# RWKV scan on one core: VectorE copies and scales for both heads, and the first two MLA weights get a pool of their own

## The chip, the core and the metric

The kernel runs on one core of a Trainium2 chip. A core has a matmul engine (TensorE, PE in the profile; PEld is its weight load), a vector engine (VectorE, DVE), a scalar engine (ScalarE, ACT), a general engine (GpSimd, POOL) and a sync engine (SyncE, SP) that here only issues DMAs. Each engine runs its own queue in order; engines wait for each other by semaphores. The metric is the device time of one execution in microseconds. Three executions of the kernel before gave a median of 4153.34 us (4151.22 to 4157.22).

## The reference, cut to what matters

Two networks run one after the other. The first has two hybrid layers; the second has four layers: an SGU mixer, an RWKV-7 mixer, an MLA attention mixer and another SGU mixer, over 512 tokens and 256 context tokens, width 1024. The change lies in the RWKV mixer's scan and at the start of the MLA mixer.

The reference's scan goes token by token in two directions (forward and flipped), 16 heads of 64 x 64 state:

```
def step(S, inp):
    w_t, k_t, v_t, kk_t, a_t = inp[:5]
    s_kk = einsum('nbhvk,nbhk->nbhv', S, kk_t)
    S = S * w_t[..., None, :] - s_kk[..., :, None] * (kk_t * a_t)[..., None, :] \
        + v_t[..., :, None] * k_t[..., None, :]
    y_t = einsum('nbhvk,nbhk->nbhv', S, inp[5])
```

MLA projects the normed hidden state `h` by columns of one matrix: `c_q, c_kv, k_rope, z = split(h @ w_in, ...)`, with 768 columns for `c_q` and then 256 for `c_kv`.

## The kernel before, in words

Everything is float32. Each weight is split into a high and a low part (`wtile`, L129): ScalarE casts (`whi`, L138), VectorE or every third time GpSimd subtracts (`wlo`, L141), and a product is three matmuls (L160).

**The scan** (`scan`, L1689). The tokens go in chunks of 64, twelve chunks (`NS`) for each of eight blocks of 128 channels (`KD`). One block holds two heads: head 0 on partitions 0 to 63, head 1 on 64 to 127, in both the VectorE inputs and the outputs. Two blocks are in flight, half a block apart: each iteration `p` of the outer loop (L1697) runs six steps of block `p` and the last six of block `p-1` side by side, two "lanes". Beside the lanes an iteration weaves in the products of the groups to come (`products`, L1774 to 1787: G, GR, TK), the triangular inverse of a later block (`inverse`, on GpSimd, L1810 to 1825, during the first iterations) with its `merge`, and the `output` of the block that was finished (L1946 to 1965, and then L160 and L999 for the output projection). PE's order there is fixed by the way the generators are woven; the other engines' orders are set by the framework's scheduler.

A lane's step (`step`, L1878): four 64-wide matmuls of G and SV (L1889); VectorE copies the result out of PSUM (`rh`, L1896); four matmuls with the inverse; their result, the chunk's update, is copied out of PSUM into `VU` (L1901 for head 0 on ScalarE, L1902 for head 1 on VectorE); four matmuls of TK and VU give the state's increment; VectorE forms the new state `st` (L1912, two instructions); the state times the next chunk's decay goes into `SV` (L1918 for head 0, two instructions on ScalarE; L1919 for head 1, one on VectorE); eight matmuls give `y`, which is copied or added into `yacc`. Both copies of a `VU` read one PSUM bank, and the framework makes L1902 wait for L1901.

The output chain: `yacc` is centred (L1949), squared on ScalarE (`ysq`, L1952), scaled (L1959), given gain and bias on ScalarE (L1961), then VectorE adds the bonus (L1963), multiplies by the gate (L1965), and after a cast on ScalarE (L177) forms the low part (L178).

**The MLA start** (`Mla.run`, L2007). Two weights of 1024 x 128 (`wkv`, L2041) come from the weight pool of the stage (two raw tiles, three high, two low). That pool is opened when the scan's pools are closed. Then `hidden` forms the normed hidden state (`hid`, `hh`, `hl`, L973 to 979, L177, L178), and the two weights multiply it.

Of the kernel before, what the change touches and what calls it, by code (L numbers as in the profile page):

```python
# [15 lines left out]
AF = mybir.ActivationFunctionType  # L16
ALU = mybir.AluOpType
# [1105 lines left out]
def flip(ap, dim):  # L1123

    a = [list(p) for p in ap.ap]
    st, n = a[dim]
    a[dim] = [-st, n]
    return bass.AP(tensor=ap.tensor, offset=ap.offset + st * (n - 1), ap=a)
# [60 lines left out]
class Rwkv:  # L1189
# [688 lines left out]
    def step(self, k, cur, s):  # L1878


        net, nc, ap = self.net, self.net.nc, self.ap
        g, q = s // 4, s % 4
        G, GR, TK, VU, SV = cur[g]
        h = [slice(0, 64), slice(64, 128)]
        de = [(d, e) for d in range(2) for e in range(2)]
        if s == 0:
            cur["y"] = ap.tile([128, S + C], F32, tag="yacc", name="yacc", bufs=3)
        TT, ps, py = cur["TT"], net.aux(), None
        mm = lambda o, d, e, a, b, first=False, last=True: nc.tensor.matmul(  # L1889
            (ps if o else py)[h[e], o * 128 + d * 64:o * 128 + d * 64 + 64], lhsT=a, rhs=b, start=first, stop=last, skip_group_check=True)  # L1890
        part = lambda o: (ps if o else py)[:, o * 128:o * 128 + 128].rearrange("p (d v) -> p d v", v=64)
        for d, e in de:
            mm(1, d, e, G[:, e, d, q, 0, :], SV[:, e, d, q, :], d == 0)
        yield
        rh = ap.tile([128, 2, 64], F32, tag="rh", name="rh", bufs=3)
        nc.vector.tensor_copy(rh, part(1))  # L1896
        yield
        for d, e in de:
            mm(2, d, e, TT[h[e], d, s, :], rh[h[e], d, :])
        yield  # L1900
        nc.scalar.copy(VU[h[0], 0, :, q, :], part(2)[h[0]])  # L1901
        nc.vector.tensor_copy(VU[h[1], 1, :, q, :], part(2)[h[1]])  # L1902
        yield
        if s < NS - 1:
            for d, e in de:
                mm(3, d, e, TK[:, e, d, q, :], VU[:, e, d, q, :])

            t = ap.tile([128, 2, 64], F32, tag="st", name="st", bufs=6)
            ec = self.ec[:, k, s]
            if s:  # L1910
                for d in range(2):
                    nc.vector.scalar_tensor_tensor(t[:, d], cur["st"][:, d], self.ec[:, k, s - 1, d:d + 1], part(3)[:, d], ALU.mult, ALU.add)  # L1912
            else:
                nc.vector.tensor_copy(t, part(3))
            cur["st"] = t
            to = cur[(s + 1) // 4][4]
            for d in range(2):
                nc.scalar.activation(to[h[0], 0, d, (s + 1) % 4, :], t[h[0], d], AF.Copy, scale=ec[h[0], d:d + 1])  # L1918
            nc.vector.tensor_tensor(to[h[1], 1, :, (s + 1) % 4, :], t[h[1]], ec[h[1], :, None].to_broadcast([64, 2, 64]), ALU.mult)  # L1919
        yield  # L1920
        py = net.aux()
        for d, e in de:
            mm(0, d, e, SV[:, e, d, q, :], G[:, e, d, q, 1, :], d == 0, False)
        for d, e in de:
            mm(0, d, e, VU[:, e, d, q, :], GR[:, d, q, e, :])
        for d in range(2):
            c = (8 + (s if d == 0 else 3 - s)) if s < 4 else (s - 4 if d == 0 else 11 - s)
            dst = cur["y"][:, c * 64:c * 64 + 64]
            if d:
                dst = flip(dst, 1)  # L1930
            if s in (2, 3) or s >= 8:
                nc.vector.tensor_tensor(dst, dst, part(0)[:, d], ALU.add)
            else:
                nc.scalar.copy(dst, part(0)[:, d])
        yield
# [65 lines left out]
class Mla:  # L2001
# [5 lines left out]
    def run(self):  # L2007
        net, nc, I, tc = self.net, self.net.nc, self.net.I, self.net.tc
# [4 lines left out]
        with ExitStack() as es:  # L2013
# [24 lines left out]
            krt = mp.tile([128, NT2, 64], F32, name="krt")  # L2038
            kr2 = mp.tile([128, NT2], F32, name="kr2")
            with net.weight_pool(2, 3, 2), net.psum(6, 2), tc.tile_pool(name="mla1", reuse_waits="tile", bufs=3) as ap:  # L2040
                wkv = [net.wcols(w_in[:, 768 + k * 128:896 + k * 128], 128) for k in range(2)]  # L2041
                hT = self.b2.hidden(i, ap, ap, True)

                raw = [ap.tile([128, T], F32, name=f"ckr{k}", bufs=1) for k in range(2)]
                for k in range(2):
                    outs = self.b2.both(True)
                    net.strip(outs, wkv[k], hT)
                    for ps, t0, t1 in outs:
                        nc.scalar.copy(raw[k][:, t0:t1], ps[:, :t1 - t0])

                outs = self.b2.both(True)
                net.strip(outs, net.wcols(w_in[:, 1024:1088], 64), hT, m=64)
                kr = ap.tile([64, T], F32, name="kr", bufs=1)
                krsq = ap.tile([64, T], F32, name="krsq", bufs=1)
                for ps, t0, t1 in outs:
                    nc.scalar.activation(kr[:, t0:t1], ps[:64, :t1 - t0], AF.Copy, scale=gr[0:64, 1:2])
                    nc.scalar.activation(krsq[:, t0:t1], ps[:64, :t1 - t0], AF.Square)
                ps = net.aux()
                for c in range(NT2):
                    nc.tensor.matmul(ps[:, c:c + 1], lhsT=krsq[:, c * 128:c * 128 + 128], rhs=net.ones[0:64, 0:1], start=True, stop=True)  # L2060
                nc.vector.tensor_copy(kr2, ps[:, :NT2])
                self.rotate(perm[0:64, 0:64], kr[:, 0:S], kr[:, 0:S], ap, 64, net.aux)
                ps = net.aux()
                for c in range(NT2):
                    nc.tensor.transpose(ps[:, c * 64:c * 64 + 64], kr[:, c * 128:c * 128 + 128], net.ident[0:64, 0:64])
                nc.scalar.copy(krt.rearrange("p c d -> p (c d)"), ps[:, :NT2 * 64])
                self.normed(raw, ckv, cols["kvn"], 256, ((0, NCH), (NCH, 2)), ap)
                rawq = [ap.tile([128, S], F32, name=f"cqr{k}", bufs=1) for k in range(6)]
                for k in range(6):
                    ps = net.acc()  # L2070
                    net.strip([(ps, 0, S)], net.wcols(w_in[:, k * 128:k * 128 + 128], 128), hT)
                    nc.scalar.copy(rawq[k], ps)
                for h in range(MH):
                    ps = net.acc()
                    net.strip([(ps, 0, S)], net.wcols(w_in[:, 1088 + h * 128:1216 + h * 128], 128), hT)
                    z = ap.tile([128, S], F32, tag="zs", name="zs", bufs=2)
                    nc.scalar.activation(z, ps, AF.Tanh, scale=0.5)
                    nc.vector.scalar_tensor_tensor(z, z, 1.0, ps, ALU.add, ALU.mult)
                    nc.sync.dma_start(zd[h * 128:h * 128 + 128, :], z)
                    if h == 0:  # L2080
                        self.normed(rawq, cq, cols["qn"], 768, ((0, NCH),), ap)
            net.drop_context()
            na, nb, nw, no = HEAD_BANKS
            with net.weight_pool(1, 3, 3), net.psum(na, nb, nw), tc.tile_pool(name="po", reuse_waits="tile", bufs=no, space=PSUM) as self.pv, \
# [382 lines left out]
```

## Time and profile before

| | |
|---|---|
| median of three executions | 4153.34 us |
| the profiled execution | 4150.81 us, of which the span 4148.8 us |
| PE busy | 3856.5 us, 93% of the span |
| PE weight load | 3194.9 us, 77% |
| DVE | 2427.8 us, 59% |
| ACT | 1592.1 us, 38% |
| POOL | 1270.4 us, 31% |
| the scan | about 2516 to 2972 us from the span's start |
| the MLA start | about 2986 to 3060 us |

The span is what the profiler sees from the first to the last instruction; 2.0 us lie around it. Shares are of the whole span, over stages with different limits, so the scan is read from its own windows. "Idle before" is the time that an engine stood still ahead of an instruction, with what ended it.

### The profile page before, as it was taken

The page shows a single profiled execution, that of the slowest core. Times are in us where ns is not written, and L with a number is a line of the kernel's source. Part 1 is how long each engine was busy: PE and PEld are TensorE (multiplying, and loading weights), DVE is VectorE, ACT ScalarE, POOL GpSimd, SP SyncE. Part 2 cuts the span into 40 slices and gives each one's busy share as a digit, 9 for nine tenths or more (in the row PEclk, how much of TensorE's full clock was granted, in tenths as well). Part 3 has the DMA queues.
Part 4 walks back from the last instruction along what each step waited for, and adds up shares of the span by engine and source line. Part 5 has one row for each costly group of instructions (what it writes and reads, how often), then busy time and mean ns, then how long its engine had stood idle before and what let it go on. Part 6 is the DMA issues. An engine that isn't in the chain of part 4 may idle for free. (4 is left out here: it accounts for less than half of the span.)

```text
span 4148.8 us, 67237 instructions
## 1 busy us (share of the span) xinstructions
PE 3856.5 (93%) x26432; PEld 3194.9 (77%) x26432; DVE 2427.8 (59%) x4769; ACT 1592.1 (38%) x3041; POOL 1270.4 (31%) x1303
## 2 busy tenths in 40 slices
PE   8999999999999999999798887888799999998999
PEld 7867777886877788888676666777577888887887
DVE  7836445774654525444566653777644788873544
ACT  4243223334322322222665532344343555553222
POOL 3321111322211312111545548860012444442221
PEclk9999999999999999999899887999889999999999
DMA  3125543122355322221347776655223122222332
GB/s 94 52 72 164 167 147 93 57 65 91 104 185 170 117 63 60 61 62 48 98 129 205 204 207 154 151 143 126 62 69 112 42 61 55 59 78 68 88 91 86
DMA packets 599016, 431.73 MB, mean 104 GB/s; under 512 B 193436, under 2 KB 532140, under 8 KB 598700
## 3 DMA queue, kind: packets, MB, share of 16 engines
q1 hardware_dynamic: 593756, 414.97, 34.8%
q0 software_dynamic: 4944, 12.46, 1.2%
q8 instruction: 209, 3.42, 0.3%
q14 instruction: 107, 0.88, 0.1%
HBM read 354.46 MB, written 68.68 MB: 102 GB/s over the span
## 5 line engine op out<-in xcount | busy, mean ns | idle before, releaser
L138 ACT CAST whi<-wraw 128x1024 fp32r<-128x1024 f32 (+3 forms) x471 | 457.2, 971 | 1167.4 <-PE acc L160 968.5
L141 POOL TENSOR_TENSOR wlo<-wraw,whi 128x1024 fp32r<-128x1024 f32 (+2 forms) x200 | 418.2, 2091 | 1246.9 <-ACT whi L138 1139.4
L160 PE MATMUL acc<-hh,whi 128*128 128x512 f32 (+2 forms) x1776 | 626.2, 377 | 9.5 <-ACT hh L421 5.0
L160 PE MATMUL acc<-hl,whi 128*128 128x512 f32 (+2 forms) x1776 | 622.1, 375 | 2.5 <-DVE hl L422 2.5
L160 PE MATMUL acc<-hh,wlo 128*128 128x512 f32 (+2 forms) x1776 | 621.3, 374 | 2.0 <-DVE wlo L141 2.0
L141 DVE TENSOR_TENSOR wlo<-wraw,whi 128x1024 fp32r<-128x1024 f32 (+3 forms) x271 | 334.2, 1234 | 438.9 <-ACT whi L138 391.1
L160 PEld LDWEIGHTS acc<-hh,whi 128*128 128x128 f32 (+1 forms) x1776 | 315.1, 188 | 84.0 <-ACT whi L138 17.3
L160 PEld LDWEIGHTS acc<-hh,wlo 128*128 128x128 f32 (+1 forms) x1776 | 315.5, 188 | 63.8 <-DVE wlo L141 2.8
L160 PEld LDWEIGHTS acc<-hl,whi 128*128 128x128 f32 (+1 forms) x1776 | 315.3, 188 | 62.6 <-DVE hl L422 4.1
L160 PE MATMUL acc<-wlo,hh 128*128 128x256 f32 (+1 forms) x896 | 297.1, 332 | 6.1 <-DVE wlo L141 6.1
L160 PE MATMUL acc<-whi,hh 128*128 128x256 f32 (+1 forms) x896 | 298.2, 335 | 2.9 <-ACT hh L978 2.3
L160 PE MATMUL acc<-whi,hl 128*128 128x256 f32 (+1 forms) x896 | 293.2, 331 | 0.0
L999 DVE SCALAR_TENSOR_TENSOR xT<-acc,mod,xT 128x512 f32<-128x512 f32 x256 | 185.6, 746 | 127.6 <-PE acc L160 126.8
L160 PEld LDWEIGHTS acc<-wlo,hh 128*128 128x128 f32 x896 | 179.0, 200 | 20.5 <-DVE wlo L141 7.1
L160 PEld LDWEIGHTS acc<-whi,hh 128*128 128x128 f32 x896 | 178.9, 200 | 20.5 <-ACT hh L978 2.9
L160 PEld LDWEIGHTS acc<-whi,hl 128*128 128x128 f32 x896 | 178.1, 199 | 14.3 <-issue 0.8
L160 PE MATMUL wide<-xsh,whi 128*128 128x512 f32 (+1 forms) x512 | 148.2, 373 | 14.7 <-ACT xsh L1383 13.7
L160 PE MATMUL wide<-xsl,whi 128*128 128x512 f32 (+1 forms) x512 | 142.8, 362 | 18.7 <-POOL xsl L1384 16.0
L160 PE MATMUL wide<-xsh,wlo 128*128 128x512 f32 (+1 forms) x512 | 141.0, 358 | 0.0
L160 PE MATMUL acc<-ffgh,whi 128*128 128x512 f32 x352 | 139.9, 400 | 0.0
L160 PE MATMUL acc<-ffgl,whi 128*128 128x512 f32 x352 | 138.4, 395 | 0.0
L160 PE MATMUL acc<-ffgh,wlo 128*128 128x512 f32 x352 | 138.3, 395 | 0.0
(626 smaller groups left out, 8726.5 us busy)
## 6 DMA issues: line engine op xcount, KB each, us to landing
ada_w<-in_ada_w SPq DMA_DIRECT2D x32, 1536.0 KB
wraw<-in_sgu_w_in SPq DMA_DIRECT2D x96, 512.0 KB
wraw<-in_w_up SPq DMA_DIRECT2D x88, 512.0 KB
wraw<-in_w_in SPq DMA_DIRECT2D x44, 512.0 KB
wraw<-in_w_down SPq DMA_DIRECT2D x32, 512.0 KB
wraw<-in_sgu_w_out SPq DMA_DIRECT2D x32, 512.0 KB
wraw<-in_rwkv_w_in SPq DMA_DIRECT2D x32, 512.0 KB
bk<-rw_bk SPq DMA_DIRECT2D x24, 512.0 KB
```

The costliest lines, as they stand in the source:

```text
L138: nc.scalar.copy(hi, raw)
L141: eng.tensor_tensor(lo, raw, hi.bitcast(F32), ALU.subtract)
L160: mm(out, lhsT=a, rhs=b[:, t0:t1], start=first and n == 0, stop=last and n == 2)
L999: nc.vector.scalar_tensor_tensor(dst[k], ps, m[:, 16 + k, j:j + 1], dst[k], ALU.mult, ALU.add)
```

## The change

In a step of the scan, VectorE makes both copies into `VU` and both products into `SV`; ScalarE makes none. Line numbers after L1902 move up by one in the new kernel (L1919 becomes L1918, L1963 becomes L1962). In MLA the first two weights are taken from a new pool on the right side of the on-chip memory with one raw, two high and two low tiles; it is closed when the stage's projections are done.

```
-        nc.scalar.copy(VU[h[0], 0, :, q, :], part(2)[h[0]])
-        nc.vector.tensor_copy(VU[h[1], 1, :, q, :], part(2)[h[1]])
+        for e in range(2):
+            nc.vector.tensor_copy(VU[h[e], e, :, q, :], part(2)[h[e]])
...
-            for d in range(2):
-                nc.scalar.activation(to[h[0], 0, d, (s + 1) % 4, :], t[h[0], d], AF.Copy, scale=ec[h[0], d:d + 1])
-            nc.vector.tensor_tensor(to[h[1], 1, :, (s + 1) % 4, :], t[h[1]], ec[h[1], :, None].to_broadcast([64, 2, 64]), ALU.mult)
+            for e in range(2):
+                nc.vector.tensor_tensor(to[h[e], e, :, (s + 1) % 4, :], t[h[e]], ec[h[e], :, None].to_broadcast([64, 2, 64]), ALU.mult)
...
+                own = net.wp, net.wbufs
+                early = ExitStack()
+                net.wp, net.wbufs = early.enter_context(tc.tile_pool(name="mlw", reuse_waits="tile", bufs=1, side="right")), (1, 2, 2)
                 wkv = [net.wcols(w_in[:, 768 + k * 128:896 + k * 128], 128) for k in range(2)]
+                net.wp, net.wbufs = own
...
+            early.close()
             net.drop_context()
```

VectorE's queue at the output chain of iteration p = 7 (`yacc` is the finished block's output, `VU`, `st` and `SV` belong to the two lanes, `rh` to their next step), before:

```order
L1959 TENSOR_TENSOR yacc<-yacc,acc 128x256
L1902 COPY VU<-aux 64x2x64
L1963 TENSOR_TENSOR yacc<-yacc,ld_b 128x768
L1902 COPY VU<-aux 64x2x64
L1912 SCALAR_TENSOR_TENSOR st<-st,rw_ec,aux 128x64 x2
L1965 SCALAR_TENSOR_TENSOR yacc<-yacc,ld_z 128x768
L1919 TENSOR_TENSOR SV<-st,rw_ec 64x2x64
L1912 SCALAR_TENSOR_TENSOR st<-st,rw_ec,aux 128x64 x2
L1919 TENSOR_TENSOR SV<-st,rw_ec 64x2x64
L178 TENSOR_TENSOR yl<-yacc,yh 128x768
L1896 COPY rh<-aux 128x128 x2
```

The same place after:

```order
L1958 TENSOR_TENSOR yacc<-yacc,acc 128x256
L1902 COPY VU<-aux 64x2x64 x4
L1962 TENSOR_TENSOR yacc<-yacc,ld_b 128x768
L1912 SCALAR_TENSOR_TENSOR st<-st,rw_ec,aux 128x64 x4
L1964 SCALAR_TENSOR_TENSOR yacc<-yacc,ld_z 128x768
L1918 TENSOR_TENSOR SV<-st,rw_ec 64x2x64 x4
L178 TENSOR_TENSOR yl<-yacc,yh 128x768
L1896 COPY rh<-aux 128x128 x2
```

All four copies of the two lanes now stand ahead of the bonus addition, where the second lane's copy stood behind it; the four products stand together behind the gate. Five of the six chains with two lanes have this order; in the one of p = 6 the `rh` copies stand ahead of L178. Elsewhere in the scan a pair of copies or products becomes four in the same place.

SP's queue of DMA issues at the end of the scan (`ld_z` is the gate of an output chain, `mcos` to `mgr` are small tables of MLA, `wraw<-in_mla_w_in 128x8x128` are the two weights, of which the first row stands last here), before:

```order
L1957 DMA ld_z<-rw_z 128x768 [waits DMAHW6_49,PE_49,Activation_49]
L135 DMA wraw<-in_rwkv_w_out 128x512 [waits DMAHW7_49,DMAHW4_49,DVE_49]
L135 DMA wraw<-in_rwkv_w_out 128x512 [waits DMAHW7_49,DMAHW0_49,DVE_49]
L1956 DMA ld_b<-rw_bonus 128x768 [waits DMAHW6_49,DMAHW1_49]
L1957 DMA ld_z<-rw_z 128x768 [waits DMAHW2_49,PE_49,Activation_49]
L2017 DMA mcos<-in_axial_cos 128x512 [waits Activation_49]
L2018 DMA msin<-in_axial_sin 128x512
L2023 DMA mgr<-in_mla_qk_gain_q 64x1 [waits DMAHW5_49]
L2023 DMA mgr<-in_mla_qk_gain_q 64x1
L2023 DMA mgr<-in_mla_qk_gain_k 64x1
L2023 DMA mgr<-in_mla_qk_gain_k 64x1 [waits DMAHW0_49]
L135 DMA wraw<-in_mla_w_in 128x8x128 [waits DMAHW1_49]
```

And after:

```order
L1955 DMA ld_b<-rw_bonus 128x768 [waits DMAHW5_49]
L1956 DMA ld_z<-rw_z 128x768 [waits DMAHW6_49,PE_49,Activation_49]
L135 DMA wraw<-in_mla_w_in 128x8x128 [waits DMAHW7_49,Pool_49]
L135 DMA wraw<-in_mla_w_in 128x8x128 [waits DMAHW7_49,DMAHW0_49,DVE_49]
L135 DMA wraw<-in_rwkv_w_out 128x512 [waits DMAHW4_49,DMAHW1_49,DVE_49]
```

The two weights' loads stand behind the gate of the last chain but one, two loads of the last projection's weights and the tables ahead of which they now go. The second waits for VectorE, which must have read the one raw tile.

ScalarE's queue at that last chain but one (`whi 128x1024` is a cast of such a weight, `whi 128x512` of the output projection's), before:

```order
L1787 COPY TK<-acc 128x512 x2
L1901 COPY VU<-aux 64x2x64
L1961 ACTIVATE yacc<-yacc,col_rwkv 128x768
L1918 ACTIVATE SV<-st,rw_ec 64x64 x2
L1934 COPY yacc<-aux 128x64 x2
L177 CAST yh<-yacc 128x768
L1901 COPY VU<-aux 64x2x64
L1918 ACTIVATE SV<-st,rw_ec 64x64 x2
```

And after:

```order
L1787 COPY TK<-acc 128x512 x2
L138 CAST whi<-wraw 128x1024
L1960 ACTIVATE yacc<-yacc,col_rwkv 128x768
L1933 COPY yacc<-aux 128x64 x2
L177 CAST yh<-yacc 128x768
L138 CAST whi<-wraw 128x1024
L138 CAST whi<-wraw 128x512 x2
```

The two casts of the weights move from the MLA start into the scan's last iteration; there the `VU` and `SV` instructions are gone from ScalarE.

## Rows read from the trace of the kernel before

**Rows 1.** Windows: us; busy us by engine with (x instructions); PE clock, DMA share, GB/s

```profile
2516.00:2972.00 456.00, 386.00 (x6688) 324.02 (x6689) 318.33 (x996) 172.83 (x540) 222.47 (x398) 0.89 0.55 128
2835.00:2888.00 53.00, 46.59 (x880) 38.77 (x882) 40.96 (x132) 22.73 (x70) 0.00 (x0) 1.00 0.50 118
2972.00:3100.00 128.00, 102.09 (x495) 83.15 (x494) 63.34 (x142) 50.71 (x86) 26.84 (x20) 0.84 0.23 64
```

**Rows 2.** Waits, 2560 to 2970 us: who waited for whom: total us, times, longest

```profile
PE aux L1889 <- DVE VU L1902: 23.6, 26, 1.8
DVE VU L1902 <- ACT VU L1901: 20.0, 20, 3.7
...
PE acc L1246 <- ACT ysq L1952: 7.8, 7, 1.2
...
PE aux L1889 <- DVE SV L1919: 5.3, 13, 0.8
```

**Rows 3.** Lines of the scan: ns min/median/max; last row: busy us, mean ns

```profile
L1902 DVE COPY VU<-aux x96: 286/295/295, 2517.4 to 2972.0; 64x128 f32<-64x128 f32 x96
...
L1919 DVE TENSOR_TENSOR SV<-st,rw_ec x88: 282/289/754, 2518.8 to 2968.9; 64x128 f32<-64x128 f32 x88
...
L1919 DVE TENSOR_TENSOR SV<-st,rw_ec 64x128 f32<-64x128 f32 x88 | 28.2, 336 | 2.3
```

**Rows 4.** Timeline of DVE, chain of p = 7: start us, us, what [idle before]

```profile
2901.75 0.29 DVE L1902 COPY VU<-aux 64x128 f32<-64x128 f32 x1
2902.87 0.96 DVE L1963 TENSOR_TENSOR yacc<-yacc,ld_b 128x768 f32<-128x768 f32 x1 [0.83 <-ACT yacc L1961]
2903.86 0.29 DVE L1902 COPY VU<-aux 64x128 f32<-64x128 f32 x1
...
2904.58 0.95 DVE L1965 SCALAR_TENSOR_TENSOR yacc<-yacc,ld_z 128x768 f32<-128x768 f32 x1
2905.56 0.29 DVE L1919 TENSOR_TENSOR SV<-st,rw_ec 64x128 f32<-64x128 f32 x1
...
2906.71 0.96 DVE L178 TENSOR_TENSOR yl<-yacc,yh 128x768 fp32r<-128x768 f32 x1
2907.58 0.48 DVE L1896 COPY rh<-aux 128x128 f32<-128x128 f32 x2
```

**Rows 5.** Timeline of PE, the same chain

```profile
2904.21 0.45 PE L1889 MATMUL aux<-VU,TK 128*64 128x64 f32 x8 [1.66 <-DVE VU L1902]
...
2907.93 0.68 PE L1889 MATMUL aux<-rh,xx 64*64 64x64 f32 x16 [0.65 <-DVE rh L1896]
```

**Rows 6.** Timeline of DVE, the stretch ahead of that chain

```profile
2896.55 0.43 DVE L1778 TENSOR_TENSOR G<-acc,rmask 64x256 f32<-64x256 f32 x1
2896.99 0.43 DVE L1779 TENSOR_TENSOR GR<-acc,rmask 128x256 f32<-128x256 f32 x1
2897.33 0.41 DVE L1778 TENSOR_TENSOR G<-acc,rmask 64x256 f32<-64x256 f32 x1
...
2898.48 0.43 DVE L1778 TENSOR_TENSOR G<-acc,rmask 64x256 f32<-64x256 f32 x1 [0.41 <-PE acc L1774]
```

**Rows 7.** Timeline of DVE and PE behind an output projection's L999, p = 3

```profile
2700.16 0.50 DVE L1902 COPY VU<-aux 64x128 f32<-64x128 f32 x2
...
2700.51 0.69 PE L1889 MATMUL aux<-VU,TK 128*64 128x64 f32 x16 [0.83 <-DVE VU L1902]
```

**Rows 8.** Timeline at the MLA start; SPq is the issue of a DMA

```profile
2939.52 0.33 SPq L1957 DMA_DIRECT2D ld_z<-rw_z  x1
...
2989.73 1.21 SPq L135 DMA_DIRECT2D wraw<-in_mla_w_in  x2
...
3016.54 0.72 ACT L978 ACTIVATE hh<-hid,mod 128x512 fp32r<-128x512 f32 x1 [9.82 <-DVE hid L973]
...
3021.01 0.80 PE L160 MATMUL acc<-hh,whi 128*128 128x512 f32 x1 [4.52 <-ACT whi L138]
...
3024.27 0.79 PE L160 MATMUL acc<-hh,wlo 128*128 128x512 f32 x1 [2.04 <-DVE wlo L141]
```

## The prediction

> **What bounds the kernel now.** The change touches two places, so I read the windows of these first. In the scan [rows 1] PE is busy 386.0 of 456 us; in the iteration from 2835 to 2888 us 46.6 of 53 us at full clock, with DVE at 41.0 and ACT at 22.7. PE bounds, DVE is close behind, and ACT has more than half its time free: the change moves work from the engine with most room to the one with least. The other window, the MLA start, shows PE 102 of 128 us busy. Then the waits [rows 2]: PE stood still 23.6 us in the scan for VectorE's copy of VU (26 times), 5.3 us for its SV, and VectorE itself 20.0 us for ScalarE's copy of VU. Last the timelines of one output chain (iteration p = 7), where the largest of these waits stand [rows 4, 5]: PE waits 1.66 us for the second lane's VU, because that copy (2903.86) stands behind the bonus addition L1963, which waits 0.83 us for ScalarE; and 0.65 us for rh, which stands behind the whole chain.
>
> **What is added and taken away.** ScalarE loses 96 copies and 176 products, none of which it was short of time for. VectorE gets 96 copies of 0.295 us and 88 products of 0.289 us (medians, [rows 3]): 28.3 + 25.4 = 53.7 us in the scan, on 318.3 us. An iteration with two lanes makes 12 steps of either kind, so 12 x 0.295 + 12 x 0.289 = 7.0 us; the iteration of [rows 1] then has 48 of 53 us on VectorE. What counts is where they fall.
>
> The distance between two of them sets their price. VectorE's neighbours overlap when they begin on the same partitions: GR at 2896.99 lasts 0.43 us, yet G, on partitions from 0 as it is, begins at 2897.33, 0.09 us before its end; while the G ahead of it, on partitions from 64, had ended (2896.98) when GR began [rows 6]. Two copies of head 1 in a row take 0.50 us, not 0.59 [rows 7]. The new copies change head each time (0, 1, 0, 1). No row shows two half-height copies on different halves, so both prices are kept: 0.32 us apart if each waits for the one before, 0.21 if they overlap. I take 0.32, since [rows 6] is the nearest row with such a change. The Trainium skill, "VectorE: DVE Perf Modes", section "Two Vector instructions with no wait between them", states this as a model: an instruction whose input or output begins in another group of 32 partitions than the last one's waits until all earlier ones have finished. It speaks for 0.32 and against this change; by it four copies take 1.25 us, by overlap 0.92.
>
> **The output chain**, with the new order, from the same start at 2901.75 [rows 4]. At 0.32: four copies end at 3.00 (all times here less 2900), the first lane's VU is whole at 2.36 (was 2.04, its head 1; +0.32) and the second's at 3.00 (was 4.15; -1.15). L1963 runs 3.03 to 3.99 (was to 3.83). Two st stood between 4.15 and 4.58, so four take some 0.85 us and end at 4.86. L1965 ends at 5.83 and the four SV at 7.1; L178 runs from 7.13 (was 6.71), and rh behind it is ready 0.4 us later than before. At 0.21 the copies end at 2.67, L1963 stays at 2.87, L1965 ends at 5.65, SV at 6.57, L178 begins at 6.6: 0.1 us earlier. So PE wins 1.15 us at the second lane's VU and has it taken back at SV and rh, which come late next: -0.1 to +0.45 us per chain; I take +0.3.
>
> **Other places of an iteration.** (a) Behind L999 of the output projection [rows 7] PE waits 0.83 us for two copies, which have become four: the second lane's is whole 0.42 to 0.75 us later, of which the first lane's matmuls cover a part: +0.3 to +0.6; I take 0.45. (b) PE waited 13 times for an SV [rows 2], about twice an iteration; the four instructions are 0.1 to 0.3 us later each: +0.2 to +0.6; I take 0.3, since part of VectorE's stretches waits for PE anyway (0.41 us ahead of a G, [rows 6]). (c) Where VectorE waits for ScalarE's VU [rows 2] the hand-over falls away. But of these 20 waits most end when PE's matmuls do, and a second copy of 0.29 us replaces ScalarE's of 0.26: -0.15 (-0.3 to 0). (d) ysq on ScalarE no longer stands behind VU copies, and PE waits for it once an iteration (7.8 us in 7): -0.1 (-0.25 to 0). Together +0.8 us an iteration (the least -0.15, the most +1.65); over six iterations with two lanes and a chain and a last with one lane, taken as half, 6.5 x 0.8 = +5.2 us (-1.0 to +10.7).
>
> Where GpSimd works beside VectorE (the first half), an SV product is dearer: 754 ns at most against a median of 289, a mean of 336 over all [rows 3]. The 88 new ones would so cost up to 4.1 us more of VectorE's time, a part of it on the path; that lies within the range above. The Trainium skill, "SBUF — State Buffer", section "Who interferes with whom", gives the reason: a Vector instruction with both inputs in the on-chip memory shares a read port with GpSimd. By it the VU copies, which read PSUM, stay at 0.295 whatever GpSimd does, and only the products of the first half are dearer.
>
> In the first two iterations there is no output chain, and ScalarE's copies of VU stand behind its long TK and xx copies: 20.0 us of VectorE's waits [rows 2] include some of these, up to 3.7 us. I take -1 us (-2 to +0.5).
>
> **The MLA start.** [Rows 8]: the first hh is ready at 3017.26 (begin 3016.54 + 0.72), yet PE's first product begins at 3021.01, 4.52 us idle for the weight's high part, and then waits 2.04 us more for the low part. With both weights split earlier these two waits end with hh and hl. The first product can begin about 3017.3: -3.7; the second wait is partly replaced by the pace at which hl arrives. I take -3.5 us (-6.6, both waits whole, to 0). VectorE and GpSimd lose a low part each in that stretch, which supports it. The loads are issued behind the gate load at 2939.52 instead of at 2989.73, 75 us ahead of use. What they displace: SP's issue of 1.21 us for both; and in the last iteration ScalarE's two casts and VectorE's low part, which stand in the queue ahead of L1961 and the st. If the load is late, they block these. ScalarE had no VU and SV left to do there, so +0.5 us (0 to +2).
>
> **Sum** against the profiled execution of 4150.8 us: +5.2 - 1 - 3.5 + 0.5 = +1.2, 4152.0 us; the ends are -1.0 - 2 - 6.6 + 0 = -9.6 and 10.7 + 0.5 + 0 + 2 = +13.2. The median of the runs stands 2.5 us above that execution, so I expect 4154.5 us, between 4144 and 4167.
>
> **Rivals.** *VectorE becomes the bound* (slower). It has 48 of 53 us to do, in an order in which four half-height instructions precede each thing that PE waits for. It decides once more than 1.9 us of the 7.0 added per iteration land on the path (6.5 x 1.9 - 4 = +8.3). With 2.4 us: 15.6 - 4 = +11.6, 4165 us. For it: the alternation at 0.32 and PE's 23.6 us of waits for this very copy; against: 12 us of free VectorE time an iteration, some of it next to those places. *The hand-over was the cost* (faster): half of PE's 23.6 us for VU goes, -12, with MLA -3.5: 4138 us. For it: the 1.66 us wait does vanish; against: rh at the chain's end, which gives it back. *The scan stays as it was*, all copies in free time, and only MLA gains: -3, 4150 us. *The early weights win nothing*, because their raw tile or their cast is held up at the scan's end: the sum without -3.5, 4158 us.
>
> **How the numbers follow.** Forecast 0.42, the scan neutral 0.10, weights in vain 0.05; VectorE the bound 0.30; the hand-over 0.13. About 0.2% (8.3 us) is what a measurement of this kernel can tell from no change. The first three lie within 8.3 us of 4153.3 but for some 0.08 of their weight, half to either side: same 0.49, faster 0.17, slower 0.34. The forecast's own range is 4144 to 4167; for eight in ten, with most of the slower case inside and half of the faster one out, I give 4141 to 4169.
>
> **What would show it.** DVE busy in the scan from 318 to about 372 us, ACT down by 73. In an output chain no more 1.66 us ahead of VU's matmuls, but more idle PE time ahead of SV and rh, and rh some 0.4 us later against L1959. The start-to-start distance of the four copies: 0.32 or 0.21. At MLA, PE's first product about 3.7 us sooner after the norm (L251), with no wait for whi. The forecast is wrong if iterations become over 1.9 us longer, or shorter by more than 1 us.

## The result, and the profile after

The changed kernel takes 4192.1 us (median of five runs, 4173.7 to 4194.6) against 4151.6 us (five runs): ratio 1.0082, 95% interval 1.0068 to 1.0095, about +34 us. I had given 4154.5 us and a range up to 4169 us. The profiled execution of the kernel after has a span of 4190.4 us, 41.6 us more than before.

The windows of the kernel after, to be set against [rows 1] (columns as there): the scan, which now ends at 3012, the iteration p = 2 and the iteration p = 6.

```profile
2516.00:3012.00 496.00, 408.26 (x6714) 337.86 (x6714) 386.99 (x1185) 106.71 (x272) 227.68 (x409) 0.87 0.52 122
2609.30:2685.30 76.00, 58.65 (x878) 48.75 (x878) 54.72 (x155) 14.42 (x37) 65.11 (x114) 0.78 0.59 130
2867.40:2922.30 54.90, 48.52 (x878) 40.08 (x878) 47.02 (x155) 14.39 (x36) 0.00 (x0) 0.97 0.47 115
```

The scan is about 40 us longer; DVE has 68.7 us more in it and ACT 66.1 us less. Of the 40 us PE spends 22.3 busy, on about the same matmuls (6688 and 6714), and 17.7 idle. An iteration is best measured from one `ysq` on ScalarE (L1952, L1951 after) to the next. Worked out from their starts in the two traces (us):

| iteration | p = 2 | 3 | 4 | 5 | 6 | 7 | 8 |
|---|---|---|---|---|---|---|---|
| GpSimd's inverse | at work | at work | at work, to 2780 | - | - | - | - |
| before | 61.2 | 56.7 | 55.4 | 56.5 | 53.0 | 46.4 | 39.7 |
| after | 76.0 | 62.6 | 62.8 | 56.7 | 54.9 | 51.0 | 41.7 |

28.1 of the 36.8 us are lost in the three iterations in which GpSimd works beside VectorE, 8.7 us in the other four. The three iterations together (columns as in [rows 1]), the kernel before and the kernel after:

```profile
2607.79:2781.13 173.34, 149.16 (x2634) 124.99 (x2634) 131.29 (x394) 68.46 (x212) 147.10 (x257) 0.92 0.62 146
2609.29:2810.71 201.42, 163.76 (x2634) 135.55 (x2634) 161.63 (x463) 42.97 (x109) 147.95 (x261) 0.86 0.56 130
```

So 13.5 of the 28.1 us are idle time of PE, and 14.6 us are the same 2634 matmuls taking longer, at a mean granted clock of 0.86 and not 0.92. What PE waits for in the idle part (waits of the kernel after, 2561 to 3008 us, columns as in [rows 2]):

```profile
PE aux L1889 <- DVE SV L1918: 23.3, 27, 2.7
PE aux L1889 <- DVE VU L1902: 16.4, 31, 1.2
DVE VU L1902 <- PE aux L1889: 11.8, 16, 1.9
...
PE acc L1246 <- ACT ysq L1951: 6.4, 7, 0.9
```

PE waits 7 us less for VU (23.6 before) and some 15 us more for SV (before, 5.3 us for VectorE's products and 3.3 us for ScalarE's). The two lines themselves: the copies cost what they did, the products do not. All to be set against [rows 3] (ns min/median/max). The copies:

```profile
L1902 DVE COPY VU<-aux x192: 271/289/297, 2517.4 to 3010.5; 64x128 f32<-64x128 f32 x192
```

the products while GpSimd works, and after it:

```profile
L1918 DVE TENSOR_TENSOR SV<-st,rw_ec x103: 273/429/2018, 2519.2 to 2815.0; 64x128 f32<-64x128 f32 x103
...
L1918 DVE TENSOR_TENSOR SV<-st,rw_ec x74: 276/287/291, 2815.0 to 3007.1; 64x128 f32<-64x128 f32 x74
```

and their busy time and mean (ns) over the scan:

```profile
L1918 DVE TENSOR_TENSOR SV<-st,rw_ec 64x128 f32<-64x128 f32 x176 | 68.9, 391 | 3.6
```

The output chain shows how. First VectorE in the chain of p = 7, where GpSimd is idle (the kernel after; it answers to [rows 4]):

```profile
2933.25 1.21 DVE L1902 COPY VU<-aux 64x128 f32<-64x128 f32 x4
2934.49 0.96 DVE L1962 TENSOR_TENSOR yacc<-yacc,ld_b 128x768 f32<-128x768 f32 x1
2935.48 0.85 DVE L1912 SCALAR_TENSOR_TENSOR st<-st,rw_ec,aux 128x64 f32<-128x64 f32 x4
2936.25 0.95 DVE L1964 SCALAR_TENSOR_TENSOR yacc<-yacc,ld_z 128x768 f32<-128x768 f32 x1
2937.12 1.23 DVE L1918 TENSOR_TENSOR SV<-st,rw_ec 64x128 f32<-64x128 f32 x4
2938.38 0.96 DVE L178 TENSOR_TENSOR yl<-yacc,yh 128x768 fp32r<-128x768 f32 x1
```

and PE in it (answers to [rows 5]):

```profile
2934.51 0.45 PE L1889 MATMUL aux<-VU,TK 128*64 128x64 f32 x8 [0.17 <-DVE VU L1902]
...
2937.54 1.31 PE L1889 MATMUL aux<-SV,G 128*64 128x64 f32 x16 [1.65 <-DVE SV L1918]
2939.60 0.68 PE L1889 MATMUL aux<-rh,xx 64*64 64x64 f32 x16 [0.74 <-DVE rh L1896]
```

The 1.66 us ahead of the second lane's VU are gone (0.17), and 1.65 us stand ahead of SV instead (before, 0.20 and 0.35 us). From the first copy to L178 it takes 5.13 us (before 4.96): what was won is given back inside the chain. Four copies or products take 1.21 to 1.23 us, that is 0.31 us from one to the next.

Now the same place in p = 2, VectorE and GpSimd together, with PE's wait:

```profile
2634.15 2.65 DVE L1918 TENSOR_TENSOR SV<-st,rw_ec 64x128 f32<-64x128 f32 x4
2634.79 0.56 POOL L1819 TENSOR_TENSOR invP<-invA,invT 96x220 f32<-96x220 f32 x1
2635.00 0.30 PE L1889 MATMUL aux<-SV,G 128*64 128x64 f32 x2 [2.70 <-DVE SV L1918]
2635.42 0.62 POOL L1821 TENSOR_TENSOR invT<-invT,invP 96x220 f32<-96x220 f32 x1
2636.11 0.53 POOL L1819 TENSOR_TENSOR invP<-invA,invT 96x207 f32<-96x207 f32 x1
2636.73 0.58 POOL L1821 TENSOR_TENSOR invT<-invT,invP 96x207 f32<-96x207 f32 x1
2636.83 1.30 DVE L178 TENSOR_TENSOR yl<-yacc,yh 128x768 fp32r<-128x768 f32 x1
```

The four products take 2.65 us, not 1.23: 0.66 us each, which is the step of GpSimd's instructions (2634.79, 2635.42, 2636.11, 2636.73). The engines take turns: each product waits for one GpSimd instruction.

Two products in a row on the same half, as the kernel before has them (head 1 of both lanes), fare otherwise. Its p = 2:

```profile
2635.48 0.59 POOL L1821 TENSOR_TENSOR invT<-invT,invP 96x192 f32<-96x192 f32 x1
2635.78 0.64 DVE L1919 TENSOR_TENSOR SV<-st,rw_ec 64x128 f32<-64x128 f32 x2
2636.14 0.62 POOL L1819 TENSOR_TENSOR invP<-invA,invT 96x175 f32<-96x175 f32 x1
```

In the single records the first of the two waits for GpSimd (0.44 us), and the second begins 0.08 us before the first ends and takes 0.28 us: no turn lies between them. After the change the halves alternate: a product begins 0.01 to 0.03 us behind the end of the one before it, and GpSimd's next instruction has begun by then (above, at 2634.79; the first product ends at 2634.85).

MLA's start, to be set against [rows 8] (kernel after):

```profile
3051.63 2.93 PE L251 MATMUL aux<-ident,rs 128*128 128x128 f32 x12 [2.47 <-DVE rs L192]
3054.60 0.72 ACT L978 ACTIVATE hh<-hid,mod 128x512 fp32r<-128x512 f32 x1 [9.81 <-DVE hid L973]
...
3055.38 0.79 PE L160 MATMUL acc<-hh,whi 128*128 128x512 f32 x1 [0.82 <-ACT hh L978]
...
3056.60 0.79 PE L160 MATMUL acc<-hl,whi 128*128 128x512 f32 x1 [0.43 <-DVE hl L979]
```

The first product follows the first hh by 0.06 us and waits for no weight.

### The profile page after: what moved, and what is told of

Its sections match the earlier page's. It is cut to its first block, busy times and chain, and to the rows that moved or that the text cites. A ratio compares the mean times of both kernels' runs of the same rounds, so it can differ in the third digit from the quotient of the medians.

```text
span 4190.4 us, 66992 instructions
## 1 busy us (share of the span) xinstructions
PE 3881.2 (93%) x26432; PEld 3208.9 (77%) x26432; DVE 2497.3 (60%) x4953; ACT 1524.8 (36%) x2769; POOL 1274.2 (30%) x1303
## 5 line engine op out<-in xcount | busy, mean ns | idle before, releaser
L999 DVE SCALAR_TENSOR_TENSOR xT<-acc,mod,xT 128x512 f32<-128x512 f32 x256 | 185.6, 746 | 124.3 <-PE acc L160 123.2
```

The source lines that it names most:

```text
L999: nc.vector.scalar_tensor_tensor(dst[k], ps, m[:, 16 + k, j:j + 1], dst[k], ALU.mult, ALU.add)
```

## The experiments

Two theories. **A**: the SV products and GpSimd's instructions take turns, and the products that wait block VectorE's queue. **B**: VectorE simply has too many instructions, 0.31 us apart, whatever they are and whoever works beside it. All ratios are against the kernel before on the same chip; "p = 2 to 4" and "p = 5 to 8" are sums of the intervals between ysq starts in each profile (before: 173.3 and 195.6 us).

**The parts one by one.** `scan_only` is the scan's edit without the MLA pool; `mla_only` the pool without the scan's edit; `vu_only` and `sv_only` are

```
-        nc.scalar.copy(VU[h[0], 0, :, q, :], part(2)[h[0]])
-        nc.vector.tensor_copy(VU[h[1], 1, :, q, :], part(2)[h[1]])
+        for e in range(2):
+            nc.vector.tensor_copy(VU[h[e], e, :, q, :], part(2)[h[e]])
```

and the corresponding edit of the SV lines, with all else as before. Expected of `scan_only`:

> The scan's edit alone, the MLA weights as before. Both theories put the whole loss here: ratio about 1.009 (+36 to +40 us against before), with the loss in iterations p = 2 to 4 (GpSimd working) some 24 us and in p = 5 to 8 some 10 us.

Of `mla_only`:

> The MLA weights' pool alone, the scan as before. Expected -1.5 to -4 us (ratio 0.9990 to 0.9997): PE's first MLA product comes sooner by about 3.5 us. If the early casts get in the way of the scan's last iteration, 0 to +3 us.

Of `vu_only`:

> VectorE makes both VU copies; the SV products stay divided as before; MLA as before. Theory A (the SV products, two inputs in the on-chip memory, are slowed by GpSimd and then block VectorE's queue): 0 to +6 us. Theory B (VectorE has too many instructions, whatever they are): about half of the loss, +15 to +20 us.

Of `sv_only`:

> VectorE makes both SV products; the VU copies stay divided as before; MLA as before. Theory A: most of the loss, +22 to +32 us, with the SV median above 400 ns while GpSimd works and 290 ns afterwards. Theory B: about half, +15 to +20 us.

| | median us (before) | ratio, 95% interval | p = 2 to 4 | p = 5 to 8 |
|---|---|---|---|---|
| scan_only | 4181.3 (4153.7) | 1.0070, 1.0058 to 1.0083 | 197.3 | 202.5 |
| mla_only | 4157.3 (4153.7) | 1.0010, 1.0001 to 1.0019 | 171.9 | 196.8 |
| vu_only | 4158.6 (4153.7) | 1.0009, 0.9997 to 1.0020 | 179.7 | 200.1 |
| sv_only | 4175.1 (4153.7) | 1.0057, 1.0045 to 1.0070 | 189.1 | 201.8 |

The products carry the loss (+24 us by the ratio, 19 to 29) and the copies little (+4 us, not clear of none). That is how A divides the loss; B's 15 to 20 us is excluded for the copies, but not quite for the products. In `sv_only` the products' median is 438 ns to 2800 us, as A has it. The parts add up, 15.8 + 6.4 against 24.0 us in p = 2 to 4. `scan_only` came out lower than expected, +29 us; with the +4 us of `mla_only` it makes the +34 us of the whole change. `mla_only` missed: no gain, but +0.4 to +8 us. Its other case, early casts in the way of the last iteration, does not show either: p = 8 takes 39.8 us (before 39.7).

Where in a group the turns fall can be read from the single records. In `scan_only` 24 groups of two products lie beside GpSimd: the first has a median of 283 ns, the second of 561, and 22 of the 24 second ones take over 400 ns. Of 28 pairs on the same half (`before`, `mla_only` and `vu_only`) only 6 second ones do. No run orders the products of a group by half, so that the alternation is what lets GpSimd in is argued from these records and not shown.

**Without GpSimd's rounds.** Both kernels of this pair leave out the inverse's rounds on GpSimd:

```
         for j in range(31):
+            if alone:
+                yield
+                continue
             n = 31 - j
             pr = work("invP", [96, 256], 1)
```

Expected of it in the kernel before:

> The kernel before without the inverse's 31 rounds on GpSimd (the inverse is left out, so the result is not the reference's; the weave keeps its length). It is the partner of scan_no_inv. Expected within 0.5% of before, -15 to 0 us, since PE, not GpSimd, bounds the scan.

and with the scan's edit:

> The scan's edit alone, without the inverse's 31 rounds on GpSimd. Theory A (GpSimd slows the products): the distance to before_no_inv is a third of the 28 us that the scan's edit costs with GpSimd at work, +8 to +14 us; the SV median is 290 ns throughout. Theory B (number of VectorE instructions and their distance of 0.31 us): the distance stays +24 to +30 us.

Measured 4142.8 us (ratio 0.9967, 0.9954 to 0.9980) and 4160.2 us (1.0011, 1.0002 to 1.0020): the scan's edit costs 17 to 18 us without GpSimd and 29 with it. In p = 2 to 4 it costs 8.6 us (163.1 to 171.7) and not 24.0; in p = 5 to 8, where GpSimd is idle in all four kernels, 10.4 (193.3 to 203.7) against 6.9, a difference that shows how far single profiles scatter. The products of `scan_no_inv` to 2800 us, median 286 ns and none over 293:

```profile
L1921 DVE TENSOR_TENSOR SV<-st,rw_ec x106: 273/286/293, 2521.8 to 2798.9; 64x128 f32<-64x128 f32 x106
```

So GpSimd's part is some 15 us by p = 2 to 4 (24.0 - 8.6) and some 11 us by the whole times (29 - 18). The total distance missed A's 8 to 14 us as it missed B's 24 to 30: both have a part, and the larger part of the 29 us is there without GpSimd.

**What in the product takes turns.** `sv_pointer` gives the decay as a scalar per partition, so that each product reads one tensor:

```
...
+            for e in range(2):
+                for d in range(2):
+                    nc.vector.tensor_scalar(to[h[e], e, d, (s + 1) % 4, :], t[h[e], d],
+                                            ec[h[e], d:d + 1], None, ALU.mult)
```

> The scan's edit, but each SV product is two VectorE instructions that take the decay as a scalar per partition in place of a second tensor (four a lane, not two); MLA as before. Theory A, if the second tensor input is what is slowed: no SV instruction over 400 ns while GpSimd works, and +10 to +18 us in place of +28, though VectorE has 176 instructions more. Theory B: more than the scan's edit, +35 us or more.

4224.8 us (4155.9), ratio 1.0164, 1.0151 to 1.0178. The products to 2800 us:

```profile
L1919 DVE TENSOR_SCALAR SV<-st,rw_ec x169: 236/463/1971, 2524.8 to 2800.0; 64x64 f32<-64x64 f32 x169
```

and eight of them in the timeline, beside GpSimd:

```profile
2644.48 3.65 DVE L1919 TENSOR_SCALAR SV<-st,rw_ec 64x64 f32<-64x64 f32 x8
2644.99 0.41 POOL L1819 TENSOR_TENSOR invP<-invA,invT 96x135 f32<-96x135 f32 x1
2645.48 0.45 POOL L1821 TENSOR_TENSOR invT<-invT,invP 96x135 f32<-96x135 f32 x1
2646.01 0.37 POOL L1819 TENSOR_TENSOR invP<-invA,invT 96x112 f32<-96x112 f32 x1
2646.46 0.42 POOL L1821 TENSOR_TENSOR invT<-invT,invP 96x112 f32<-96x112 f32 x1
2646.96 0.33 POOL L1819 TENSOR_TENSOR invP<-invA,invT 96x87 f32<-96x87 f32 x1
```

My version of A, that the second tensor is what is slowed, fell: half as much data with one tensor takes turns just the same, a turn for each instruction. The total, +68 us, lies on B's side. Turns are only a part of it: against `scan_only` this kernel is 20.8 us longer in p = 2 to 4 (218.0) and also 14.5 us longer in p = 5 to 8 (216.9), where GpSimd is idle and the instructions are merely more. `sv_psum` then takes the state from PSUM: VectorE writes the state a second time there, with an instruction pair like L1912's, and the products read that copy (the edit is against the kernel after).

```
...
+            t2 = part(0)
+            if s:
+                for d in range(2):
+                    nc.vector.scalar_tensor_tensor(t2[:, d], cur["st"][:, d],
+                        self.ec[:, k, s - 1, d:d + 1], part(3)[:, d], ALU.mult, ALU.add)
...
-                nc.vector.tensor_tensor(to[h[e], e, :, (s + 1) % 4, :], t[h[e]], ...
+                nc.vector.tensor_tensor(to[h[e], e, :, (s + 1) % 4, :], t2[h[e]], ...
```

> The scan's edit, but VectorE writes the new state a second time, into a free quarter of the step's PSUM bank (176 instructions of 0.28 us more), and the SV products read that copy: one tensor from PSUM, one from the on-chip memory; MLA as before. Theory A1 (VectorE and GpSimd take turns on a path into the on-chip memory that an instruction with one such tensor at ordinary rate does not use): no SV instruction over 320 ns while GpSimd works; p = 2 to 4 lose less than the 24 us of the scan's edit although VectorE makes more. Theory A2 (any Vector instruction that reads the on-chip memory takes turns): SV median above 400 ns as before. Total by A1 +20 to +35 us (the second states cost, the turns are gone), by A2 +45 us or more.

4220.3 us (4155.0), ratio 1.0161, 1.0144 to 1.0178. The products to 2800 us:

```profile
L1924 DVE TENSOR_TENSOR SV<-aux,rw_ec x94: 271/289/295, 2528.1 to 2796.2; 64x128 f32<-64x128 f32 x94
```

and four of them in the timeline, beside GpSimd:

```profile
2640.41 1.24 DVE L1924 TENSOR_TENSOR SV<-aux,rw_ec 64x128 f32<-64x128 f32 x4
2640.90 0.53 POOL L1819 TENSOR_TENSOR invP<-invA,invT 96x207 f32<-96x207 f32 x1
2641.51 0.58 POOL L1821 TENSOR_TENSOR invT<-invT,invP 96x207 f32<-96x207 f32 x1
```

No product over 295 ns: A1's mechanism holds. Its total, +20 to +35 us, does not (+67 us), nor does its claim that p = 2 to 4 lose less than the scan's edit: the second states cost more than the turns. In p = 5 to 8 this kernel is 21.2 us longer than `scan_only` (223.7 against 202.5), in p = 2 to 4 only 2.9 us (200.2 against 197.3), where the turns are saved.

**Shorter GpSimd instructions.** `short_inv` cuts each of the inverse's multiplications and subtractions, while it has four rows or more, into four (`for a, b in cut: eng.tensor_tensor(pv[:, a:b], ...)`).

> The scan's edit, but each GpSimd instruction of the inverse is cut into four over a quarter of the elements; MLA as before. If an SV product waits for the GpSimd instruction that is running, its median while GpSimd works falls from 464 ns to 340 to 400 ns. The total is open, since GpSimd's own work grows: +15 to +45 us against before. If the products are slowed by GpSimd's load as such, the median stays at 450 ns or more.

4247.9 us (4155.0), ratio 1.0223, 1.0207 to 1.0239. The products' median fell to 290 ns, further than expected; GpSimd's rows show nearly twice the work (370 us, 198 in the kernel after), so its work on the inverse ends at 2928 us and not at 2780. PE then waits 12.6 us for the inverse (`xx<-rw_mt`) and 32.2 us for a load of G, so the total says nothing of the turns. GpSimd's rows (2516 to 3090 us; busy us, mean ns, idle before):

```profile
L1825 POOL TENSOR_TENSOR invT<-invT,invP 96x60 f32<-96x60 f32 (+28 forms) x729 | 191.7, 291 | 1.8
L1821 POOL TENSOR_TENSOR invP<-invA,invT 96x60 f32<-96x60 f32 (+29 forms) x728 | 178.4, 273 | 14.5
```

and the products to 2800 us:

```profile
L1922 DVE TENSOR_TENSOR SV<-st,rw_ec x82: 274/290/1878, 2522.2 to 2789.4; 64x128 f32<-64x128 f32 x82
```

The median leaves next to no wait, and the trace shows why: with short instructions it is mostly GpSimd that waits. Its instructions have a median of 330 ns beside a product and of 262 ns with VectorE idle. Four of them without products beside them, and four beside four products:

```profile
2723.91 0.87 POOL L1821 TENSOR_TENSOR invP<-invA,invT 96x26 f32<-96x26 f32 x4
2725.74 1.35 POOL L1821 TENSOR_TENSOR invP<-invA,invT 96x27 f32<-96x27 f32 x4
2725.76 1.19 DVE L1922 TENSOR_TENSOR SV<-st,rw_ec 64x128 f32<-64x128 f32 x4
```

So the price of a turn goes with the length of the GpSimd instruction in the way, and either engine can be the one that pays.

**The other way round.** `sv_act` gives ScalarE the products of both heads and VectorE none.

> The other way round: ScalarE makes the SV products of both heads (four instructions a lane of 0.33 us), VectorE none; the VU copies stay divided; MLA as before. Theory A: VectorE is relieved of 88 products, of which the contended ones were dear, but a lane's SV needs 1.3 us on ScalarE: -5 to +5 us. Theory B (VectorE's load decides): -15 to -20 us.

4162.0 us (4155.9), ratio 1.0011, 1.0003 to 1.0020. Freeing VectorE of its products gains nothing; B's -15 us did not come. Why is open: a lane's four products do stand one behind the other on ScalarE, 0.34 us each, but PE waits for SV no longer than before (3.5 us over 2611 to 2972, before 8.4), and what grew is PE's busy time from 2516 us to the last `ysq`, 414.4 us against 388.7, at a granted clock of 0.86 against 0.89. No version tried beats the kernel before.

## Why the prediction was wrong

Two terms of the sum failed, and the MLA start with them. The experiments put about 11 us of the loss to the turns, where the sum had nothing beyond its range, 18 us to the scan's edit without them, where it had 4.2, and 4 us to the MLA pool, where it had -3.0. Each of these measured parts is uncertain by some 5 us.

The first step that failed is the term for GpSimd's presence, where I sized it: "88 new ones would so cost up to 4.1 us more of VectorE's time, a part of it on the path". I took the mean of [rows 3], 336 ns, as what a product costs beside GpSimd. That mean was mostly of single products and of pairs on one half, most of which were hardly held: of the 48 that overlapped a GpSimd instruction in the trace before, the median was 298 ns. In the new groups only the first product can come so cheaply: GpSimd's next instruction has begun when one product has ended, and the next product waits for it. In the trace after, 82 overlap, with a median of 541 ns, and all of a group stand ahead of what PE waits for. In VectorE's time the term measured 14 us where I had at most 4.1: by the rows, 176 x (391 - 289) ns = 18.0 us against 88 x (336 - 289) ns = 4.1 us before. In the kernel's time it came to the 11 to 15 us above; of the 15, by p = 2 to 4, 8 us are idle time of PE and 7 us slower matmuls. The row for it was there, a maximum of 754 ns for an instruction of 289; I read it as a rare case and not as the price of a turn.

The second step that failed is (b), the wait for SV, which has its numbers under "other places" below, together with a clock that no term held. Both waits were named in the prediction and came out several times larger. The rival that comes nearest, "VectorE becomes the bound", was at 4165 us still 27 us short.

The Trainium skill, "SBUF — State Buffer", section "Who interferes with whom", which I cited for that term, states the mechanism: the path that VectorE and GpSimd share is an exclusive lock. The turns of 0.66 us and GpSimd's own wait in `short_inv` agree. The Trainium skill lists there `tensor_scalar` too among the operations that can contend, in its two-port modes, when the operands meet their conditions; the products of `sv_pointer` were held (median 463 ns), and those of `sv_psum`, with PSUM as one input, were not (at most 295 ns).

Point by point:

- *Distance of the copies.* 0.32 us was right: 1.21 us for four, 0.31 us apart.
- *The output chain.* Right in kind (the wait moves from VU to SV and rh) and a little smaller than taken: from the first copy to L178 +0.17 us, where the working had +0.42 and I took +0.3 for the chain.
- *The other places without GpSimd.* Taken at +0.8 us an iteration in all; p = 5 to 8 show +8.7 us in the profile after, +6.9 in `scan_only` and +10.4 in the pair without GpSimd, about +2 each. A single sum: I forecast +5.2 us for these iterations without turns, and the pair measured 17 to 18 for the whole scan. PE's wait for SV is the mis-sized part here, term (b): without GpSimd it is 18.7 us in `scan_no_inv` against 4.2 + 2.8 in `before_no_inv` (VectorE's and ScalarE's products), +11.7 where I had +0.3 an iteration; VU gave back 6.8 (20.4 to 13.6). The rival "VectorE becomes the bound" set its limit at 1.9 us an iteration, so without turns the kernel would have gone about that way (17 to 18 us over 6.5 iterations is 2.7 each).
- *PE's clock.* No term of mine held that the same matmuls could take longer (in p = 2, at a granted clock of 0.78 and not 0.89, 878 of them took 58.7 us of PE's time and not 50.3). In p = 2 to 4 that is half of the loss: 14.6 of 28.1 us in the kernel after, 11.9 of 24.0 in `scan_only` (0.87, 0.92 before) and 5.1 of 8.6 in the pair without GpSimd (0.94, 0.96 before). PE was idle for longer in all three, by 13.5, 12.0 and 3.7 us; that the idle time brings the lower clock is not shown, and `sv_act` has a lower clock there (0.90) with less idle time (19.5 us, 24.2 before).
- *The MLA start.* PE's first product came 3.75 us after L251 began instead of 7.45, the 3.7 us forecast. Of these some 1.4 us are left at the end of the stretch (from L251 to its next instructions 64.26 us before, 62.81 after): with its weights ready PE waits for hh and hl instead (4.0 us in six waits over 3017 to 3080 in `mla_only`; before 6.6 in two). I had taken -3.5 us, less 0.5 for what the loads displace. In the time of the whole kernel no gain shows (+0.4 to +8 us for `mla_only`); where that comes from is open.
- *The first two iterations.* I took -1 us; p = 2 began 1.5 us later in the kernel after, 0.4 us earlier in `scan_only` and, with the old scan, 3.3 us later in `mla_only`. Single profiles scatter too much to tell.

## What to carry to other kernels

Before work is moved to VectorE, see what GpSimd does beside it, and look at the maximum of such an instruction in the trace, not at its median or mean: a single instruction often slips through, but in a group in which each begins behind the end of the one before, nearly every one after the first paid a GpSimd instruction. The copies and products that read PSUM were not held by GpSimd here (at most 297 and 295 ns); the products whose data all lie in the on-chip memory were. All of them still take their place in VectorE's queue: without GpSimd's rounds the scan's edit cost 17 to 18 us, more than the turns added. And a wait that a change removes in a chain must be followed to the chain's last instruction, on the engine that now carries the work.

## What the runs showed of the hardware that was not expected

VectorE products with their data in the on-chip memory, each begun behind the end of the one before, alternate with GpSimd's instructions one for one: 0.66 us each at GpSimd's step of 0.62 to 0.69, 0.46 us on average (3.65 for eight) at a step of 0.45 on average, whether they read two tensors of 64x128 elements or one of 64x64 and a scalar. Of two products on the same half the second begins 0.08 us before the end of the first, and mostly passed without a turn (22 of 28 took under 400 ns). Short GpSimd instructions are themselves held by the products (four in 1.35 us, not 0.87). With the state in PSUM there is no turn (1.24 us for four beside GpSimd, 1.23 without it).
